# Stacking the two input parts into one 512-column product in half of a block's projections

## The chip, the cores and the metric

The kernel runs on one core of a Trainium2 chip. The core has five engines that run side by side and meet at semaphores: TensorE (PE in the profile, with its weight loads as PEld), VectorE (DVE), ScalarE (ACT), GpSimd (POOL) and SyncE (SP, which here only issues transfers). The metric is the device time of one execution in microseconds (us). Before the change the median of three runs is 792.66 us (792.65 to 792.79).

## What is computed

One layer of a streaming encoder on 256 frames (T = 256) of width 1024: a SwiGLU network, a mixing block, a cross-attention over a memory of 256 frames, and a second SwiGLU network. The mixing block is the part that matters here:

```
h = RMSNorm(x)
q_a, f_a, i_a, g_a, q_b, k_b, v_b, f_b, gates = split(h @ w_in)
A = gated linear recurrence of (q_a, f_a, i_a), 8 heads of 128
B = forgetting attention of (q_b, k_b, v_b, f_b), 8 heads of 128
y = sigmoid(gate_A) * (norm(A) * silu(g_a)) @ w_branch_a + sigmoid(gate_B) * B @ w_branch_b
x = x + RMSNorm(y @ w_out)
```

f_a are the forget gates, f = lb + (1 - lb) * sigmoid(f_a). The attention adds a running sum of log forget values to its scores. The cross-attention's queries are h @ w_mq, with h the next norm of x. Everything is float32.

## The kernel before

**Two parts for every operand.** TensorE is fed with numbers of a shorter float type (fp32r). Every operand is therefore split in two: hi is its rounded value, lo is what the rounding left. A product of x and w is the sum hi·hi + hi·lo + lo·hi, three products that accumulate in one PSUM bank. Weights arrive from memory as blocks of 128 x 1024 float32 (`load_split`, L130 to 145): SyncE issues the transfer into a `raw` tile, ScalarE casts it to `hi` (L142), VectorE subtracts to get `lo` (L144). There are four `raw` tiles and eight pairs of `hi` and `lo`; one *chunk* is four such blocks, the 1024 x 512 weights of 512 output columns. The activations' two parts lie in a class `Pair`: tiles `hT` and `lT`, transposed, with 256 frames as the free dimension. `gain_split` (L285, L286) writes them.

**Two kinds of projection.** `proj_tok` leaves frames on the partitions: 24 products of 512 columns for 128 frames and 512 outputs, the activations as the loaded operand. `proj_col` leaves outputs on the partitions: for 128 outputs and 256 frames, eight steps (kb) of three products of 256 columns, in which the weights are the loaded operand:

```python
MM(ps[:, a:b], wh, X.hi(kb)); MM(..., wh, X.lo(kb)); MM(..., wl, X.hi(kb))
```

`proj_col2` does this for two blocks of 128 outputs side by side in one PSUM bank of the ring `mm` (two banks). It is used for the forget gates f_a, the recurrence's queries q_a, the attention's k_b and q_b, the memory's keys mk and the memory queries mq. PSUM has eight banks in three rings: `mm` (2), `tr` (2, transposes) and `acc` (4).

**The order of the mixing block.** In the program's text: i_a; f_a (two chunks); q_a (two chunks); g_a with the attention's forget logit (three narrow chunks of 344 columns, `load_split(gf_in...)`); then k_b, q_b of the first four heads (c = 0) and k_b, q_b of the last four (c = 1); v_b; the gates; the branch projections. The recurrence is done in parallel over frames: class `Rec` (two of them, four heads each) builds products for distances 0, 1, 2, 4, ..., 128 in six *sets*, (0, 1), (2, 4), (8, 16), (32), (64), (128). Each set is: small products on TensorE into one or two `acc` banks (`products`), multiplications of K and Q in place on VectorE (`grow`, L705 and L715), copies by ScalarE of half of K (`gather`, L681) or of Q (`stash`, L685), and at the end `keep`, which copies the products out of PSUM into the score matrix (VectorE L729 and L734, ScalarE L743 to L751). A set needs the K and Q that the set before has grown. In the profile K is `k`, Q is `qf` (before its growth `q`), the gathered copy `early`, the small score matrix and the pairwise products of forget gates `aux` and `tq`, and the finished score matrix `f`. The sets stand in the text behind k_b and q_b, but with a mark: `after(r0 + R_AT[si])` with R_AT = (52, 126, 210, 254, 298, 344) gives them priority and lets them issue from that many products after the start of the g_a projection.

**What decides the order.** A planner takes the recorded instructions and lays each engine's list out by priority and by its estimate of when things are ready. A tile of a ring gets its buffer when an older tile of that ring has been released, and tiles of one ring get their buffers in the order of the text. Each engine then runs its list strictly in order.

**Behind the recurrence** stand the products of the score matrices with the inputs `iv` (called O below; L834 to 846: 24 products into four `acc` banks, which a norm and a product with `Gt`, L846, read), and the attention. Its scores are made in two groups of queries, each for two groups of heads, from k_b and q_b; VectorE adds the forget sums `cbc` and `cbm` (L883, L885). `cbm` is a broadcast of 8 x 256 numbers to 128 partitions, 512 KB, which GpSimd fetches (L857) and masks (L860); its tile takes a buffer of the general ring `m4`, and GpSimd's list holds the clearing of the score matrices (L723, `grow(1)`) ahead of it.

Of the kernel before, what the change touches and what calls it, by code (L numbers as in the profile page):

```python
# [11 lines left out]
F32 = mybir.dt.float32  # L12
F32R = mybir.dt.float32r
I32 = mybir.dt.int32
AF = mybir.ActivationFunctionType
ALU = mybir.AluOpType
AX = mybir.AxisListType

P = 128
D = 1024  # L20
T = 256
KB = D // P
# [57 lines left out]
def block_kernel(ctx: ExitStack, tc: tile.TileContext, wts, head_in, gf_in, x_in, mem_in, memT_in, cols, rows, fbias, masks, out):  # L80
    nc = tc.nc
    V, S, G, PE = nc.vector, nc.scalar, nc.gpsimd, nc.tensor
# [4 lines left out]
    sp = ctx.enter_context(tc.tile_pool(name="small", bufs=8))  # L87
# [5 lines left out]
    def MM(*args, **kw):  # L93
        log.append(PE.matmul(*args, **kw).ins)  # L94
# [9 lines left out]
    def nm(s):  # L104
        count[0] += 1
        return f"{s}_{count[0]}"

    def m4(shape, dt=F32, n="m"):
        return mp.tile(shape, dt, tag="m4", name=nm(n))
# [4 lines left out]
    def acc():  # L114
        return pp.tile([P, 512], F32, tag="acc", name=nm("acc"), bufs=4)

    def mm():
        return pp.tile([P, 512], F32, tag="mm", name=nm("mm"), bufs=2)
# [34 lines left out]
    def chunk(name, c):  # L153
        return [unit(name, 4 * c + i) for i in range(4)]

    def blk(units, kb, n=512):
        hi, lo = units[kb // 2]
        o = (kb % 2) * 512
        return hi[:, o : o + n], lo[:, o : o + n]

    def split(hi, lo, src):
        a = S.copy(hi, src)
        b = V.tensor_tensor(out=lo, in0=src, in1=hi.bitcast(F32), op=ALU.subtract)  # L163
        return a.ins, b.ins

    class Pair:


        def __init__(self, n=2):
            self.h, self.l = [], []  # L170
            for _ in range(n):
                self.more()
# [5 lines left out]
        def hi(self, kb, a=0, b=T):  # L178
            return self.h[kb // 4][:, kb % 4, a:b]

        def lo(self, kb, a=0, b=T):
            return self.l[kb // 4][:, kb % 4, a:b]

    def proj_tok(ps, X, units, h, n=512):

        a, b = h * P, h * P + P
        for kb in range(KB):
            wh, wl = blk(units, kb, n)
            MM(ps, X.hi(kb, a, b), wh, start=(kb == 0), stop=False)
            MM(ps, X.hi(kb, a, b), wl, start=False, stop=False)  # L190
            MM(ps, X.lo(kb, a, b), wh, start=False, stop=(kb == KB - 1))

    def proj_col(ps, X, units, cb):

        a, b = cb * P, cb * P + P
        for kb in range(KB):
            wh, wl = blk(units, kb)
            MM(ps, wh[:, a:b], X.hi(kb), start=(kb == 0), stop=False)
            MM(ps, wh[:, a:b], X.lo(kb), start=False, stop=False)
            MM(ps, wl[:, a:b], X.hi(kb), start=False, stop=(kb == KB - 1))  # L200

    def proj_col2(X, units, cbs):
        ps = mm()
        for j, cb in enumerate(cbs):
            proj_col(ps[:, j * T : (j + 1) * T], X, units, cb)
        return ps.rearrange("p (c t) -> p c t", c=2)

    def bc(a, shape, dim):
        return a.unsqueeze(dim).to_broadcast(shape)
# [54 lines left out]
    def fac_of(i, h):  # L264
        return fac[i][:, 32 * h : 32 * h + 1]
# [4 lines left out]
    def row_of(cols2):  # L270

        runs = sp.tile([P, 64], F32, tag="runs", name=nm("runs"), bufs=1)
        V.transpose(runs, cols2)
        rd = dp.tile([2, 4, 32], F32, name=nm("rd"))
        G.dma_start(rd.rearrange("h k t -> k h t"), runs[0:P:32].rearrange("k (h t) -> k h t", h=2))
        row = sp.tile([P, T], F32, tag="row", name=nm("row"), bufs=2)
        G.dma_start(row, rd.rearrange("h k t -> (h k t)").partition_broadcast(P))
        return row
# [204 lines left out]
    for kb in range(KB):  # L483
# [7 lines left out]
        if kb % 2 == 0 or kb == 1:  # L491
            a, b = ((0, 512), (512, D))[kb] if kb < 2 else (0, D)
# [8 lines left out]
    for kb in range(KB):  # L501
# [3 lines left out]
        for c in range(2):  # L505
            hi, lo = (p[:, kb % 2 * 512 : kb % 2 * 512 + 512] for p in cache[_AT["f1_in"] + 4 * c + kb // 2])
# [13 lines left out]
            nc.sync.dma_start(fb_s, fbias)  # L520
        return [rstd_x(x_halves(h)) for h in range(2)]

    X2 = Pair()
    r2 = [None, None]

    def half(X, r, h, g, *ms, into=None):

        for i, m in enumerate(ms):
            with after(m):
                to_T(X, x_blocks(h), h, g, (i,) if len(ms) == 2 else (0, 1))  # L530
        r[h] = rstd_x(x_halves(h), into)

    ffn("f1_in", "f1_dn", X1, norm_1, 0, 0, lambda m: half(X2, r2, 0, G_MIX, m + L_F1, into=fac_of(0, 0)))


    iv = [m4([P, 2, 512], n="iv") for _ in range(2)]
    for h in range(2):
        m = len(log)
        for c in range(2):
            ps = mm()  # L540
            if h == 0 and c == 1:
                behind.extend(evicted)
            u = chunk("i_a", c)
            behind.clear()
            proj_tok(ps, X2, u, h)
            iv_last = S.activation(iv[c][:, h, :], ps, AF.Copy, scale=r2[h]).ins
        if h == 0:
            half(X2, r2, 1, G_MIX, m + L_IA, into=fac_of(0, 1))
    row2 = row_of(fac[0])
# [18 lines left out]
    def heads_of(t, j):  # L568

        return t[:, :, 2 * j : 2 * j + 2].rearrange("p b h t -> p h b t")  # L570

    def halves(ps):
        return ps.rearrange("p h (b t) -> p h b t", b=2)

    row2h = row2.rearrange("p (b t) -> p b t", b=2)
    fT, kT_, qT_ = [], [], []
    for c in range(2):
        u = chunk("f_a", c)
        f, k = m4([P, 2, 4, P], n="f"), m4([P, 2, 4, P], n="k")
        for j in range(2):  # L580
            fj = heads_of(f, j)
            ps = proj_col2(X2, u, (2 * j, 2 * j + 1))
            V.tensor_tensor(out=fj, in0=halves(ps), in1=bc(row2h, [P, 2, 2, P], 1), op=ALU.mult)
            S.activation(fj, fj, AF.Sigmoid)
            for i in (2 * j, 2 * j + 1):
                hd = 4 * c + i
                V.tensor_scalar(out=f[:, :, i], in0=f[:, :, i], scalar1=olb[:, hd : hd + 1], scalar2=lbv[:, hd : hd + 1], op0=ALU.mult, op1=ALU.add)
        V.tensor_scalar(out=k, in0=f, scalar1=-1.0, scalar2=1.0, op0=ALU.mult, op1=ALU.add)
        fT.append(f)
        kT_.append(k)  # L590
    for c in range(2):
        u = chunk("q_a", c)
        q = m4([P, 2, 4, P], n="q")
        for j in range(2):
            qj = heads_of(q, j)
            ps = proj_col2(X2, u, (2 * j, 2 * j + 1))
            z = sp.tile([P, 2, 2, P], F32, tag="z2", name=nm("z2"), bufs=3)
            V.tensor_tensor(out=z, in0=halves(ps), in1=bc(row2h, [P, 2, 2, P], 1), op=ALU.mult)
            S.activation(qj, z, AF.Sigmoid)
            V.tensor_tensor(out=qj, in0=qj, in1=z, op=ALU.mult)  # L600
        qT_.append(q)
# [156 lines left out]
    for c in range(3):  # L758
        u = [load_split(gf_in[4 * c + i], GF) for i in range(4)]
        n = min(GF, D - c * GF)  # L760
        for h in range(2):
            ps = mm()
            proj_tok(ps[:, :GF], X2, u, h, GF)
            sg = sp.tile([P, 512], F32, tag="z2", name=nm("z2"), bufs=3)[:, :n]
# [31 lines left out]
    for c in range(2):  # L796
        for name, lst, sc in (("k_b", kb_, 1.0), ("q_b", qb_, 1.0 / math.sqrt(128.0))):
            u = chunk(name, c)
            t = m4([P, 4, T], n=name)
            m = len(log)  # L800
            for j in range(2):
                ps = proj_col2(X2, u, (2 * j, 2 * j + 1))
                for i in range(2):
                    V.scalar_tensor_tensor(out=t[:, 2 * j + i], in0=ps[:, i], scalar=sc, in1=row2, op0=ALU.mult, op1=ALU.mult)
            lst.append(t)
            if c == 0 and name == "k_b":
                forget(m + 46)
# [27 lines left out]
    for h in range(2):  # L835
        ps = [acc(), acc()]
        for hd in range(8):
            g, i = hd // 4, hd % 4
# [16 lines left out]
    for g in range(2):  # L855
        t = m4([P, 4, T], n="cbm")
# [68 lines left out]
    for c in range(2):  # L925
        u = chunk("v_b", c)
        t = m4([P, 2, 512], n="v_b")
        for h in range(2):
            ps = mm()
# [65 lines left out]
    for c in range(2):  # L995
        for name, X, zc in (("br_a", OA, c), ("br_b", OB, 2 + c)):
            u = chunk(name, c)
            for h in range(2):
                z = zs[zc][:, h]
                m = len(log)  # L1000
                ps = mm()
# [16 lines left out]
                for i, (xx, w) in enumerate(((X.hi(kb, a, b), wh), (X.hi(kb, a, b), wl), (X.lo(kb, a, b), wh))):  # L1018
                    MM(ps[n], xx, w[:, ns], start=(kb == 0 and i == 0), stop=(kb == KB - 1 and i == 2))

    X3 = Pair()
    r3 = [None, None]
    po = [[acc(), acc()], [acc(), acc()]]
    m = len(log)
# [11 lines left out]
    KM, QM, VM = Pair(0), Pair(0), Pair(0)  # L1036
    m = len(log)
    for c in range(2):
        u = chunk("mk", c)
        KM.more()  # L1040
        for j in range(2):
            js = slice(2 * j, 2 * j + 2)
            ps = proj_col2(M, u, (2 * j, 2 * j + 1))
            t = sp.tile([P, 2, T], F32, tag="z2", name=nm("km"), bufs=3)
            V.tensor_tensor(out=t, in0=ps, in1=bc(rowm, [P, 2, T], 1), op=ALU.mult)
            split(KM.h[c][:, js], KM.l[c][:, js], t)
            if j == 0:
                half(X3, r3, c, G_MEM, m + (L_WO, L_MK)[c], m + (L_WO, L_MK)[c] + 16)
    for c in range(2):
        u = chunk("mq", c)  # L1050
        QM.more()
        for j in range(2):
            js = slice(2 * j, 2 * j + 2)
            ps = proj_col2(X3, u, (2 * j, 2 * j + 1))
            split(QM.h[c][:, js], QM.l[c][:, js], ps)

    def mem_v(c):
        u = chunk("mv", c)
# [189 lines left out]
```

## Time and profile before

| | |
|---|---|
| median of 3 runs | 792.66 us |
| profiled execution | 792.24 us, its span 790.4 us |
| PE busy | 782.3 us, 4736 instructions |
| PEld busy | 677.6 us |
| DVE, ACT, POOL busy | 519.2, 426.7, 13.4 us |
| weights cast (L142), subtracted (L144) | 262.2 us of ACT, 306.6 us of DVE, 256 each |
| column products of 256 columns (`mm<-hT,hi`, `mm<-lT,hi`, `mm<-hT,lo`) | 384 of each: six projections, 48 blocks of 128 outputs, 8 steps each; 284 ns each as drawn |

The profile is one execution. The span runs from the first to the last instruction; the time of the execution is 1.84 us longer. A product's drawn length reaches into the next one, so the pitch (start to start) is what a product costs in a row of products, and it is read from the chain of waits, which cuts the execution into pieces of one engine. A product of two operands in plain float32 (the recurrence, the attention's scores) appears as two instructions.

### The profile page before, as it was taken

The numbers are of one execution on the slowest core, as the hardware profiler recorded it, in microseconds if no ns is written. First come the engines' busy times: TensorE is split into PE (matmuls) and PEld (weight loads), VectorE is DVE, ScalarE is ACT, GpSimd is POOL, SyncE is SP. The second block draws the span as 40 slices with busy tenths as digits, with TensorE's granted clock in tenths as the row PEclk, the third lists the DMA queues.
The fourth block names the chain that finished last, engine by engine and source line by source line (L and its number), as shares of the span: only waits on it lengthen the run. The fifth ranks groups of instructions, "written<-read, shape, count | busy, mean of one in ns | idle before, by whom it ended". The sixth has DMA issues, their size and how long they took to land.

```text
span 790.4 us, 12205 instructions
## 1 busy us (share of the span) xinstructions
PE 782.3 (99%) x4736; PEld 677.6 (86%) x4736; DVE 519.2 (66%) x826; ACT 426.7 (54%) x656; POOL 13.4 (2%) x36
## 2 busy tenths in 40 slices
PE   9999999999999999999999999999999999999996
PEld 7888888888899999998788888999888888888885
DVE  6774545557767899488686666964669754545543
ACT  7654444546664677357774345643647644444541
POOL 0000000000000102100000000000000000000000
PEclk9999999999999999999999999999999999999999
DMA  9775654563664547634576655455164655654521
GB/s 350 245 266 212 225 189 160 187 210 110 198 209 143 180 136 221 260 120 152 197 246 226 210 189 163 168 184 178 63 230 134 230 197 207 208 197 161 186 81 54
DMA packets 44345, 147.82 MB, mean 187 GB/s; under 512 B 5048, under 2 KB 8768, under 8 KB 44288
## 3 DMA queue, kind: packets, MB, share of 16 engines
q1 hardware_dynamic: 43168, 144.83, 53.9%
q0 software_dynamic: 688, 1.85, 0.9%
q8 instruction: 37, 0.61, 0.3%
q10 hardware_dynamic: 432, 0.37, 0.1%
q14 instruction: 20, 0.16, 0.1%
HBM read 145.97 MB, written 1.06 MB: 186 GB/s over the span
## 4 chain that ended last, share of the span: by engine, by line
PE 98%; DMA 1%; DVE 0%; ACT 0%; issue 0%; SPq 0%; DVEq 0%; ACTq 0%
PE mm L94 67%; PE acc L94 27%; PE tr L369 1%; PE tr L94 1%; PE tr L294 1%; DMA head<-in_head_dram 1%; PE tr L900 0%; PE tr L991 0%; PE acc L1101 0%; DVE xs L350 0%; DVE post L340 0%; ACT hi L509 0%; SPq L493 0%; ACT hT L285 0%; SPq L488 0%
## 5 line engine op out<-in xcount | busy, mean ns | idle before, releaser
L144 DVE TENSOR_TENSOR lo<-raw,hi 128x1024 fp32r<-128x1024 f32 (+1 forms) x256 | 306.6, 1206 | 122.4 <-ACT hi L142 114.3
L142 ACT CAST hi<-raw 128x1024 fp32r<-128x1024 f32 (+1 forms) x256 | 262.2, 1039 | 149.6 <-PE mm L94 82.2
L94 PE MATMUL mm<-lo,hT 128*128 128x512 f32 (+1 forms) x592 | 227.2, 386 | 0.0
L94 PE MATMUL mm<-hi,hT 128*128 128x512 f32 (+1 forms) x592 | 227.0, 386 | 0.0
L94 PE MATMUL mm<-hi,lT 128*128 128x512 f32 (+1 forms) x592 | 226.8, 386 | 0.0
L94 PEld LDWEIGHTS mm<-hi,hT 128*128 128x128 f32 x592 | 111.2, 188 | 21.4 <-ACT hT L285 0.3
L94 PEld LDWEIGHTS mm<-hi,lT 128*128 128x128 f32 x592 | 111.3, 188 | 21.4 <-DVE lT L286 0.2
L94 PEld LDWEIGHTS mm<-lo,hT 128*128 128x128 f32 x592 | 111.1, 188 | 20.6
L94 PE MATMUL acc<-hi,act 128*128 128x512 f32 x352 | 111.9, 391 | 0.0
L94 PE MATMUL mm<-hT,lo 128*128 128x256 f32 x384 | 109.2, 284 | 0.0
L94 PE MATMUL mm<-hT,hi 128*128 128x256 f32 x384 | 109.0, 284 | 0.0
L94 PE MATMUL mm<-lT,hi 128*128 128x256 f32 x384 | 109.0, 284 | 0.0
L94 PEld LDWEIGHTS acc<-hi,act 128*128 128x128 f32 x352 | 66.0, 188 | 13.6 <-DVE act L163 0.4
L94 PEld LDWEIGHTS mm<-hT,hi 128*128 128x128 f32 x384 | 73.7, 192 | 0.1
L94 PEld LDWEIGHTS mm<-lT,hi 128*128 128x128 f32 x384 | 73.7, 192 | 0.1
L94 PEld LDWEIGHTS mm<-hT,lo 128*128 128x128 f32 x384 | 73.7, 192 | 0.1
L94 PE MATMUL acc<-lo,act 128*128 128x512 f32 x176 | 69.8, 398 | 0.0
L374 ACT ACTIVATE sg<-mm,rstd 128x256 f32<-128x256 f32 x40 | 19.0, 475 | 75.5 <-PE mm L94 75.5
L379 DVE SCALAR_TENSOR_TENSOR at<-mm,rstd,sg 128x256 f32<-128x256 f32 x40 | 19.2, 480 | 57.4 <-ACT sg L374 57.4
L94 PEld LDWEIGHTS acc<-lo,act 128*128 128x128 f32 x176 | 33.1, 188 | 6.1
L94 PE MATMUL acc<-hi,hT 128*128 128x512 f32 x96 | 35.1, 392 | 0.7 <-ACT hi L509 0.4
L94 PE MATMUL acc<-hi,lT 128*128 128x512 f32 x96 | 35.1, 393 | 0.0
(199 smaller groups left out, 655.1 us busy)
## 6 DMA issues: line engine op xcount, KB each, us to landing
raw<-in_wts_dram SPq DMA_DIRECT2D x247, 512.0 KB, 4.4
raw<-in_gf_dram SPq DMA_DIRECT2D x12, 344.0 KB, 3.9
head<-in_head_dram SPq DMA_DIRECT2D x7, 392.0 KB, 6.5
grow<-in_rows_dram SPq DMA_DIRECT2D x4, 512.0 KB, 5.9
xs<-in_x_dram SPq DMA_DIRECT2D x2, 512.0 KB, 7.8
cbm<-cd POOLq DMA_DIRECT2D x2, 512.0 KB, 9.7
brow<-in_rows_dram SPq DMA_DIRECT2D x4, 256.0 KB, 4.9
memT<-in_memT_dram SPq DMA_DIRECT2D x2, 512.0 KB, 5.3
```

The lines of the kernel that those rows point to most:

```text
L94: log.append(PE.matmul(*args, **kw).ins)
L142: S.copy(h, r)
L144: V.tensor_tensor(out=l, in0=r, in1=h.bitcast(F32), op=ALU.subtract)
L294: PE.transpose(ps[:, j * P : (j + 1) * P], src(kb), ident)
L369: PE.transpose(trv[:, j, h * P : (h + 1) * P], ats[c, h][:, j * P : (j + 1) * P], ident)
L374: silu = S.activation(sg, ps[:, :FC], AF.Silu, scale=r2[h])
L379: V.scalar_tensor_tensor(out=a, in0=ps[:, FC:], scalar=r2[h], in1=sg, op0=ALU.mult, op1=ALU.mult)
```

## The change

Class `Joined` replaces `Pair` for the activations of the mixing block (X2) and of the memory queries (X3): the two parts of one kb lie side by side, so that `both(kb)` is 512 columns, hi then lo. `proj_both` multiplies the weights' first part with both in one product and the weights' second part with hi alone. One block of 128 outputs now takes a whole bank: its left half collects hi·hi + lo·hi, its right half the weights' first part times the activations' second. `added` puts them together. It is used for f_a, q_a, k_b and q_b of c = 1, and mq. k_b and q_b of c = 0 and mk stay with `proj_col2`. All of the new blocks take their bank from `acc`.

```diff
+    def proj_both(ps, X, units, cb):
+        a, b = cb * P, cb * P + P
+        for kb in range(KB):
+            wh, wl = blk(units, kb)
+            if kb == KB - 1:
+                MM(ps[:, :T], wl[:, a:b], X.hi(kb), start=False, stop=False)
+            MM(ps, wh[:, a:b], X.both(kb), start=(kb == 0), stop=(kb == KB - 1))
+            if kb < KB - 1:
+                MM(ps[:, :T], wl[:, a:b], X.hi(kb), start=False, stop=False)
+
+    def added(out, ps):
+        two = len(out.shape) == 3
+        lo = sp.tile([P, T], F32, tag="c1", name=nm("plo"), bufs=7)
+        S.copy(lo, ps[:, T:])
+        a, b = (t.rearrange("p (b t) -> p b t", b=2) if two else t for t in (ps[:, :T], lo))
+        V.tensor_tensor(out=out, in0=a, in1=b, op=ALU.add)
...
-    X2 = Pair()
+    X2 = Joined()
...
-            ps = proj_col2(X2, u, (2 * j, 2 * j + 1))
-            V.tensor_tensor(out=fj, in0=halves(ps), in1=bc(row2h, [P, 2, 2, P], 1), op=ALU.mult)
+            for i in (2 * j, 2 * j + 1):
+                ps = acc()
+                proj_both(ps, X2, u, i)
+                added(f[:, :, i], ps)
+            V.tensor_tensor(out=fj, in0=fj, in1=bc(row2h, [P, 2, 2, P], 1), op=ALU.mult)
...
-            ps = proj_col2(X2, u, (2 * j, 2 * j + 1))
             z = sp.tile([P, 2, 2, P], F32, tag="z2", name=nm("z2"), bufs=3)
-            V.tensor_tensor(out=z, in0=halves(ps), in1=bc(row2h, [P, 2, 2, P], 1), op=ALU.mult)
+            for i in range(2):
+                ps = acc()
+                proj_both(ps, X2, u, 2 * j + i)
+                added(z[:, i], ps)
+            V.tensor_tensor(out=z, in0=z, in1=bc(row2h, [P, 2, 2, P], 1), op=ALU.mult)
...
-                ps = proj_col2(X2, u, (2 * j, 2 * j + 1))
+                if c == 0:
+                    ps = proj_col2(X2, u, (2 * j, 2 * j + 1))
+                else:
+                    for i in range(2):
+                        ps = acc()
+                        proj_both(ps, X2, u, 2 * j + i)
+                        added(t[:, 2 * j + i], ps)
+                    ps = t[:, 2 * j : 2 * j + 2]
...
-    X3 = Pair()
+    X3 = Joined()
...
-        for j in range(2):
-            js = slice(2 * j, 2 * j + 2)
-            ps = proj_col2(X3, u, (2 * j, 2 * j + 1))
-            split(QM.h[c][:, js], QM.l[c][:, js], ps)
+        for i in range(4):
+            ps = acc()
+            proj_both(ps, X3, u, i)
+            hi, lo = QM.h[c][:, i], QM.l[c][:, i]
+            S.copy(hi, ps[:, :T])
+            t = sp.tile([P, T], F32, tag="c1", name=nm("qm"), bufs=7)
+            V.tensor_tensor(out=t, in0=ps[:, :T], in1=hi.bitcast(F32), op=ALU.subtract)
+            V.tensor_tensor(out=lo, in0=ps[:, T:], in1=t, op=ALU.add)
```

More of the change, by code (lines that the diff above doesn't have):

```diff
@@ L182, in lo, with __init__, hi, both @@
             return self.l[kb // 4][:, kb % 4, a:b]
+    class Joined:
+        def __init__(self):
+            self.t = [m4([P, 2, 2, T], F32R, "hlT") for _ in range(KB // 2)]
+        def hi(self, kb, a=0, b=T):
+            return self.t[kb // 2][:, kb % 2, 0, a:b]
+        def lo(self, kb, a=0, b=T):
+            return self.t[kb // 2][:, kb % 2, 1, a:b]
+        def both(self, kb):
+            return self.t[kb // 2][:, kb % 2].rearrange("p s t -> p (s t)")
+    def proj_both(ps, X, units, cb):
[13 more added lines that the diff above has]
+        V.tensor_tensor(out=out, in0=a, in1=b, op=ALU.add)
     def proj_tok(ps, X, units, h, n=512):
@@ L570, in heads_of @@
         return t[:, :, 2 * j : 2 * j + 2].rearrange("p b h t -> p h b t")
-    def halves(ps):
-        return ps.rearrange("p h (b t) -> p h b t", b=2)
     row2h = row2.rearrange("p (b t) -> p b t", b=2)
```

## The prediction

> **What bounds the kernel now.** I read the shares of busy time first, then the chain that ended last, then its pieces.
>
> ```profile
> PE 782.3 (99%) x4736; PEld 677.6 (86%) x4736; DVE 519.2 (66%) x826; ACT 426.7 (54%) x656; POOL 13.4 (2%) x36
> PEclk9999999999999999999999999999999999999999
> PE 98%; DMA 1%; DVE 0%; ACT 0%; issue 0%; SPq 0%; DVEq 0%; ACTq 0%
> ```
>
> PE works from 7.8 us to 783.8 us almost without a stop, at the full granted clock, and is 98% of the chain. So only two things can move the time: the pitch of PE's products, and stops of PE that are not there now. The pieces of the chain (start us, length us, what) that the sum needs:
>
> ```profile
> 45.14 10.90 PE mm L94 x48
> ...
> 268.53 1.81 PE acc L94 x122
> 270.34 11.87 PE mm L94 x74
> 282.21 1.28 PE acc L94 x86
> 283.49 8.50 PE mm L94 x64
> 292.00 0.22 PE tr L780 x2
> 292.21 2.38 PE mm L94 x20
> 294.60 1.33 PE acc L94 x108
> 295.92 5.46 PE mm L94 x44
> 301.39 0.69 PE acc L94 x50
> 302.08 5.46 PE mm L94 x44
> 307.55 1.08 PE acc L94 x32
> 308.63 5.71 PE mm L94 x46
> 314.34 1.79 PE acc L94 x16
> 316.13 21.95 PE mm L94 x183
> 338.08 5.36 PE acc L94 x48
> ...
> 347.09 0.22 PE tr L94 x2
> ...
> 497.82 7.66 PE mm L94 x64
> ```
>
> The six `acc` pieces from 268.53 to 314.34 are the recurrence's sets, 7.98 us together. Between two of them lie 11.87, 11.10, 5.46, 5.46 and 5.71 us of projection products, and in that time DVE and ACT grow K and Q without PE standing still.
>
> **What it removes.** 48 products of 512 columns take 10.90 us, a pitch of 0.2271; 64 products of 256 columns take 7.66, a pitch of 0.1197. A step kb was 3 x 0.1197 = 0.3591 and becomes 0.2271 + 0.1197 = 0.3468, so 0.0123 less. There are 32 changed blocks (f_a 8, q_a 8, k_b and q_b of c = 1 together 8, mq 8) with 8 steps each: 256 steps, **-3.1 us**. All of it lies on PE and so on the path. The Trainium skill, "TensorE: Matmul & The Clock Gate", section "Back-to-back issue gap", gives N / 2.4 + 2.5 ns for a product of N columns. By it the saving would be one fixed 2.5 ns per step, 0.64 us in all; the rows' pitches, 0.1197 and 0.2271, lie 10 to 11 ns above its 109.2 and 215.8, so the rows decide.
>
> **What it adds.** For 24 blocks ACT copies a half bank (128x256), DVE adds it, and DVE's multiplication by the row reads SBUF; mq has one ACT copy and two DVE operations per block. The nearest rows:
>
> ```profile
> L374 ACT ACTIVATE sg<-mm,rstd 128x256 f32<-128x256 f32 x40 | 19.0, 475 | 75.5 <-PE mm L94 75.5
> L804 DVE SCALAR_TENSOR_TENSOR k_b<-mm,row 128x256 f32<-128x256 f32 x8 | 3.0, 414 | 1.7 <-PE mm L94 1.7
> ```
>
> Per block 0.48 of ACT and 0.41 of DVE, in a time of 8 x 0.3468 = 2.77 us on PE. In the windows (us, then busy time of PE, PEld, DVE, ACT, POOL)
>
> ```profile
> 214.00:260.00 46.00, 46.00 (x385) 46.00 (x384) 32.03 (x45) 25.79 (x32) 0.00 (x0) 1.00 0.52 170
> ...
> 306.00:345.00 39.00, 39.00 (x346) 38.50 (x346) 25.73 (x41) 18.79 (x29) 6.41 (x10) 1.00 0.68 234
> ...
> 780.00:790.00 10.00, 3.76 (x17) 2.79 (x15) 3.57 (x10) 1.63 (x6) 0.00 (x0) 0.94 0.30 105
> ```
>
> f_a and q_a (the first) leave DVE 14 us and ACT 20 us free of 46, and four `acc` banks let a block wait three blocks, 8.3 us, for its eviction. I cost these at nothing; the bounds are 0 and one late eviction per chunk, 8 x 0.41 = 3.3. mq's last block is read by PE over 3 us after its end: nothing.
>
> **What it moves.** This decides. The new blocks take `acc` banks, and banks of a ring are given in the order of the text. The blocks of k_b and q_b with c = 1 stand in the text ahead of the recurrence's sets, so no set can have a bank until seven of these eight blocks have theirs. In the changed kernel's instruction list PE's order there is (products, kinds):
>
> ```
> 112+1 k_b, q_b c=1 | 96 sets 0,1 | 15 k_b, q_b | 16 | 3 v_b | 48 sets 2,4 | 10 v_b | 7 fox scores | 9 v_b
> | 64 sets 8,16 | 2 v_b | 16 | 1 v_b | 16 set 32 | 4 v_b | 8 set 64 | 14 v_b | 4 set 128 | 8 set 64 | 5 v_b
> | 4 set 128 | 1 fox score | 24 O | 21 v_b | ...
> ```
>
> Where 74, 84, 44, 44 and 46 products lay between the sets, there are now 18, 26, 3, 4 and 14. PE has little to do while DVE grows K and Q. The rows for that growth:
>
> ```profile
> 302.45 0.67 DVE L705 TENSOR_TENSOR k<-k,aux 128x512 f32<-128x512 f32 x1
> 303.05 0.67 DVE L705 TENSOR_TENSOR qf<-qf,aux 128x512 f32<-128x512 f32 x1
> ```
>
> ```profile
> L142 ACT CAST hi<-raw 128x1024 fp32r<-128x1024 f32 x24 | 24.2, 1046 | 19.0 <-PE mm L94 14.1 <-DMA raw<-in_wts_dram 4.8
> L681 ACT COPY early<-k 128x512 f32<-128x512 f32 x8 | 4.9, 636 | 1.8 <-DVE k L705 1.8
> L743 ACT COPY f<-aux 32x256 f32<-32x256 f32 x8 | 3.2, 403 | 0.1
> L748 ACT COPY f<-acc 64x256 f32<-64x256 f32 x4 | 1.5, 367 | 1.6 <-PE acc L94 1.6
> ```
>
> ```profile
> L734 DVE COPY_PREDICATED aux<-masks_s,acc 128x128 f32<-128x128 int32 x10 | 2.8, 368 | 0.0
> L885 DVE SCALAR_TENSOR_TENSOR p<-tr,ct,cbm 128x128 f32<-128x128 f32 x8 | 2.2, 341 | 0.7 <-issue 0.7
> ```
>
> One multiplication follows another after 0.60 us. With T0 the start of set 0 (near 324 us), by hand (estimates, each from these rows):
> - Sets 0, 1 end at 1.9. Eight multiplications (4.8) and two smaller products (0.7) later sets 2, 4 end at 7.4. PE's work in between is 15 products (2.55), 3 (0.68) and the sets' 1.28: idle **1.0**.
> - Sets 8, 16 need a bank that DVE frees with its copies of sets 0 and 1, 14 operations behind (eight at 0.60, the others near 0.3): 13.85, so the sets end at 15.35. Some ACT copies that DVE waits for stand behind weight casts of 1.05 us. Of these 7.95 us, PE fills 19 v_b products (4.31), 7 scores (1.54) and 1.33: idle **0.75**.
> - Set 32 ends at 17.55 behind its multiplications, PE filling 3 products and 0.69: **0.8**. The first half of set 64 ends at 19.3, filled by 4 products and 0.54: **0.3**.
> - At 19.1 DVE comes to the first addition with `cbm` (L885). On POOL's queue the fetch of `cbm` stands behind 12 clearings, and its buffer is that of the old q tile, which the products of set 8 read until 14.5:
>
> ```profile
> 271.91 3.05 POOL L723 MEMSET f<- 64x256 f32 x12 [63.72 <-ACT early L681]
> 310.57 1.10 POOL L857 DMA_DIRECT2D cbm<-cd  x2
> 318.95 1.27 POOL L860 TENSOR_SCALAR_AFFINE_SELECT cbm<-cbm 128x512 f32<-128x512 f32 x2 [7.28 <-DMA cbm<-cd]
> ```
>
> ```profile
> DMA to landing us min/median/max: 8.3/9.7/11.1
> ```
>
>  The clearings end by about 9. The fetch issues at 14.5, lands 8.3 later (the smaller value: the first of the two landed so), and two selections (1.27) make it 24.2. In DVE's queue the last multiplications for sets 64 and 128 wait behind that addition: four additions, a reduction, K and Q later, at 27.1, set 128 can start. PE's 14 products (3.2) end at 22.5: idle **4.85**.
> - Set 128 and the rest of set 64 end at 31.75: **0.95**. O waits for 13 ACT copies (0.37 to 0.40 each, from 29.6); with its 5.36 it ends at 38.8: **1.5**.
> - Behind it the second fox scores wait for O's banks, which the norm and L846 free, and their transposes for copies: **1.35**.
>
> The sum is 11.5 us of idle. PE's work is not changed by the moving. SP's list keeps its order; its transfers wait for `raw` tiles, which the casts among ACT's copies free, and the row below shows what each then needs. With four in flight I cost that at nothing, since PE's stops delay what reads the weights by as much; the bound is one transfer.
>
> ```profile
> raw<-in_wts_dram SPq DMA_DIRECT2D x247, 512.0 KB, 4.4
> ```
>
> Bounds of the idle: without the wait for `cbm` and with shorter hops 5.3; with a landing of 11.1 and 0.15 more on some 20 hops 17. A gain from the moving is excluded: PE now idles only at the two ends, 8 us together.
>
> **The sum.** The profiled execution took 792.24, 0.42 below the median. 792.24 - 3.1 + 11.5 = 800.6; against the median, **801.0**.
>
> **The rivals.**
> - *The recurrence still fits under its cover* (the other side). If the growth between sets ran beside v_b and the fox scores, with less than 1.5 us of idle, the saving would stay: 789.5 to 791. It decides at 3.1 us of idle. For it: PE never idled there before, and 48 v_b products (10.9) remain. Against: some 24 multiplications in a row at 0.60 are 14.4 us alone, and copies and `cbm` come on top. Chance 0.04; idle of 1.5 to 4.7, which gives within 0.2% of before (1.6 us, what a measurement of this kernel can tell), 0.03.
> - *The chain only*: `cbm` arrives in time, because the readers of the q tile end earlier or the fetch lands sooner, and no other wait takes its place: idle 5 to 8. For it: O could not start before ACT's 13 copies anyway. Against: what then ends last is again the chain of multiplications, and the waits behind O grow when it comes earlier. This gives 794.6 to 797.6. Chance 0.12.
> - *Longer*: the landing takes 11.1, the hops are slower, or the clock falls. In the window 780 to 790, where PE has stops, the granted clock is 0.94. If PE ran at half speed after its long stop, the 2.5 us of work behind it would double, less 0.95 idle that it fills: +1.6, 802.6; with the landing 805.4. The Trainium skill, same page, "Part 1: The HAM clock gate", says that a window of some 3.4 us without work halves the clock; this rule speaks against the change, and the 0.94 is the only trace of it here. Chance 0.19 for 803.5 to 807.
> - *The change doesn't do what it says*: 512 columns with two halves of one bank cost as much as two of 256 (no row shows a product of 512 into a bank that 256-column products also write): no 3.1, 804.1. It lies in the case before.
>
> **How the numbers follow.** The forecast, idle of 8 to 14 us, 797.6 to 803.5, has 0.60; the time is its middle, 801.0. Chain only 0.12, longer 0.19 (above 807 another 0.02), within 0.2% 0.03, faster 0.04. The range 795.0 to 806.4 takes in the two bounds of the idle (5.3 and 17, less 3.1) and leaves out some 0.13. Slower is 0.93.
>
> **What would show it.** Products of 512 columns into `acc` from hlT at a pitch of 0.227, and 4480 products in PE's count. PE's share of the chain under 98%, with DVE, ACT and POOL in it. Sets behind k_b and q_b in the chain, with PE idle between q_b and O: about 10 us in a stretch of 39. DVE idle before L885's addition, ended by POOL, some 5 us. The prediction falls if PE stays busy there, if the 3.1 is not seen before 300 us, or if the long stop has another cause than `cbm`.

## The result, and the profile after

The changed kernel takes 796.70 us (median of five runs, 796.49 to 798.06) against 792.66 before. The ratio is 1.0059 (95% interval 1.0048 to 1.0070): slower by 0.5 to 0.7%. The profiled execution took 796.49, with a span of 794.7.

The page of the changed kernel: PE's load, and the chain by engine.

```profile
PE 782.6 (98%) x4480; PEld 662.8 (83%) x4480; DVE 531.7 (67%) x862; ACT 434.2 (55%) x684; POOL 13.9 (2%) x36
PE 90%; DVE 5%; ACT 2%; issue 1%; DMA 1%; SPq 0%; POOL 0%; DVEq 0%; POOLq 0%; ACTq 0%
```

256 products are gone (4480 instructions), and PE's share of the chain has fallen from 98% to 90%. PE's busy time has not fallen, although it does less: a product is drawn longer than it takes (0.39 us for one of 512 columns, against a start-to-start time of 0.23), so a stop of 0.15 us behind a product is counted as busy.

PE's timeline shows where the recurrence's sets stand now (start, length, shapes; in brackets the idle time ahead and what ended it). Line numbers of the changed kernel are higher by 34 to 44 (L742 is L705 of before, L901 is L857, L929 is L885).

```profile
325.02 1.29 PE L94 MATMUL acc<-q,k 128*32 128x32 f32 x126
...
330.53 0.46 PE L94 MATMUL acc<-q,early 128*32 128x32 f32 x32 [0.87 <-ACT q L722]
...
341.36 0.46 PE L94 MATMUL acc<-qf,k 128*32 128x32 f32 x32 [0.27 <-DVE qf L742]
...
343.68 0.69 PE L94 MATMUL acc<-qf,k 128*64 128x64 f32 x16
...
348.40 1.77 PE L94 MATMUL acc<-qf,k 128*128 128x128 f32 x24 [0.63 <-DVE qf L742]
...
351.76 1.13 PE L94 MATMUL acc<-qf,k 128*128 128x128 f32 x8 [0.24 <-DVE qf L742]
...
355.48 1.35 PE L94 MATMUL acc<-iv,f 128*128 128x128 f32 x10 [1.09 <-issue]
...
359.94 0.48 PE L94 MATMUL mm<-hi,hlT 128*128 128x512 f32 x1
```

All six sets stand between 325 and 353, behind k_b and q_b. PE is drawn idle ahead of three of them (0.87, 0.27 and 0.63 us), inside the last (0.24) and inside O (1.09). In the kernel before, the same rows began at 268, and no stop of PE was drawn between 160 and 560 us.

The longer pieces of its chain around `cbm` (short ones between them are left out), and the answer on that tile:

```profile
337.06 2.09 PE mm L94 x9
339.15 0.44 PE acc L94 x32
339.63 0.48 issue
340.13 4.19 DMA cbm<-cd
344.46 0.63 POOL cbm L904
345.38 0.86 DVE p L929 x3
346.24 0.91 DVE k L742
347.15 0.59 DVE mx L930
347.74 0.61 DVE qf L742
348.40 1.17 PE acc L94 x8
```

```profile
L901 POOL DMA_DIRECT2D cbm<-cd x2: 547/552/558, 340.1 to 340.7; - x2
...
DMA to landing us min/median/max: 4.2/4.7/5.2
```

The end of set 8's products releases the fetch of `cbm`, the fetch releases the selections, these release DVE's additions, and behind them come the multiplications for set 128. Every link of the predicted chain is there; the landing took 4.2 us, half of the 8.3 that were forecast. The windows say why it could be quick:

```profile
306.00:325.00 19.00, 19.00 (x109) 16.28 (x107) 12.64 (x21) 7.20 (x12) 0.00 (x0) 1.00 0.65 222
325.00:340.00 15.00, 14.13 (x474) 11.83 (x475) 14.52 (x33) 11.04 (x18) 2.71 (x12) 1.00 0.02 4
340.00:360.00 20.00, 17.63 (x237) 14.35 (x223) 17.10 (x39) 15.03 (x46) 3.99 (x6) 1.00 0.30 107
```

The last two columns are the DMA engines' share and GB/s; the one ahead of them is the granted clock, 1.00 in all three. The weights' transfers had stopped (4 GB/s from 325 to 340), and `cbm` had the queues almost to itself. (It is two transfers of 512 KB, 1 MB in all, and not 512 KB.) In the kernel before, between 310.5 and 323 us, 2.58 MB of weights moved beside it, and `cbc`, another broadcast of 512 KB, had been issued 0.87 us ahead of it. In the five kernels of this document with late sets, the first of the two transfers lands in 4.2 to 4.4 us; in the eight with the sets among the products, in 7.9 to 9.3. No run changes the traffic alone, but one transfer speaks for the weights as the cause: in the changed kernel `cbc` is fetched at 296.85, with weights beside it and no other broadcast above 4 KB, and takes 8.3 us.

**How runs are compared below.** The first transfers land at different times: the first transposition of the first network starts at 32.0 to 34.2 us from one execution to the next, whatever the kernel. Two profiled executions are therefore compared from that instruction on. In the kernel before and the changed kernel it and the transpositions of G (`Gt`), which have the same work ahead of them in both, are these rows:

```profile
32.24 0.60 PE L369 MATMUL tr<-ident,at 128*128 128x128 f32 x4
...
371.48 1.03 PE L294 MATMUL tr<-ident,G 128*128 128x128 f32 x8
```

```profile
32.17 0.60 PE L403 MATMUL tr<-ident,at 128*128 128x128 f32 x4
...
376.09 1.03 PE L328 MATMUL tr<-ident,G 128*128 128x128 f32 x8
```

With the second transposition of X2's source (`xs`, near 200 us) and the last product of the second network, counted from that first row, in us:

| kernel | X2 | G | last product | against before |
|---|---|---|---|---|
| before | 168.32 | 339.24 | 751.13 | |
| changed | 169.00 | 343.92 | 755.47 | +4.34 |
| new tiles, old products | 169.00 | 339.88 | 752.06 | +0.93 |
| f_a, q_a, mq joined | 169.05 | 338.75 | 750.34 | -0.79 |
| changed, c = 1 in banks of mm | 168.98 | 338.15 | 749.78 | -1.35 |
| the same, tiles of kb and kb + 4 | 168.30 | 337.49 | 748.79 | -2.34 |

All kernels of the table are in the experiments. The +4.34 of the change comes apart into +0.93 for the new tiles, -2.28 for the products (749.78 against 752.06, same tiles and same order) and +5.69 for the late sets (755.47 against 749.78, same tiles and products).

### The profile page after: what moved, and what is told of

It reads as the page before. It is cut to its first block, busy times and chain, and to the rows that moved or that the text cites. A ratio compares the mean times of both kernels' runs of the same rounds, so it can differ in the third digit from the quotient of the medians.

```text
span 794.7 us, 11754 instructions
## 1 busy us (share of the span) xinstructions
PE 782.6 (98%) x4480; PEld 662.8 (83%) x4480; DVE 531.7 (67%) x862; ACT 434.2 (55%) x684; POOL 13.9 (2%) x36
## 4 chain that ended last, share of the span: by engine, by line
PE 90%; DVE 5%; ACT 2%; issue 1%; DMA 1%; SPq 0%; POOL 0%; DVEq 0%; POOLq 0%; ACTq 0%
PE mm L94 52%; PE acc L94 35%; PE tr L403 1%; DVE lo L144 1%; PE tr L94 1%; ACT junk L284 1%; PE tr L328 1%; DMA head<-in_head_dram 1%; DMA cbm<-cd 1%; DVE post L351 1%; ACT f L780 0%; DVE hlT L320 0%; PE tr L944 0%; DVE xs L355 0%; DVE k L742 0%
## 5 line engine op out<-in xcount | busy, mean ns | idle before, releaser
L94 PE MATMUL mm<-lo,hT 128*128 128x512 f32 x416 | 161.3, 391 | 0.0
L94 PE MATMUL mm<-hi,hT 128*128 128x512 f32 x416 | 161.1, 390 | 0.0
L94 PE MATMUL mm<-hi,lT 128*128 128x512 f32 x416 | 160.8, 390 | 0.0
L94 PE MATMUL mm<-hi,hlT 128*128 128x512 f32 (+1 forms) x352 | 104.2, 374 | 0.0
L94 PE MATMUL acc<-hlT,hi 128*128 128x512 f32 x256 | 88.3, 397 | 0.0
L94 PEld LDWEIGHTS mm<-hi,hlT 128*128 128x128 f32 x352 | 64.3, 188 | 9.6
L94 PE MATMUL acc<-hlT,lo 128*128 128x256 f32 x256 | 66.7, 281 | 0.0
L94 PE MATMUL mm<-lo,hlT 128*128 128x512 f32 (+1 forms) x176 | 65.8, 374 | 0.4 <-DVE lo L144 0.4
L94 PEld LDWEIGHTS acc<-hlT,hi 128*128 128x128 f32 x256 | 46.1, 188 | 8.7
L94 PEld LDWEIGHTS acc<-hlT,lo 128*128 128x128 f32 x256 | 48.3, 189 | 2.9
```

## The experiments

Theory A was that the late place of the recurrence's sets costs the time. Rival B was that the new products cost it, with their copies and additions.

**The place, with the products kept or left out.** First, c = 1 back to the old form:

```diff
-                if c == 0:
+                if True:
                     ps = proj_col2(X2, u, (2 * j, 2 * j + 1))
```

> k_b and q_b of c = 1 go back to two blocks of 256-column products in one bank of mm; f_a, q_a and mq stay joined. Theory A (the late place of the recurrence's sets costs the time, because the new blocks take acc banks ahead of them): the sets return to their old place, nothing stops PE there, and 192 steps save 0.0066 us each (0.3525 in the changed kernel's trace, 0.3591 before): 1.3 less, with up to 0.6 more for what delays PE near 198 us: 791.4 to 792.0. Rival B (the new products with their copies and additions cost the time, wherever they stand): three quarters of the added 4.0 us stay, 795.7.

Measured 791.79, ratio 0.9992 (0.9984 to 1.0001). Second, the new form in another ring:

```diff
                     for i in range(2):
-                        ps = acc()
+                        ps = mm()
                         proj_both(ps, X2, u, 2 * j + i)
```

> The changed kernel, but the joined blocks of k_b and q_b with c = 1 take their banks from the ring mm, one bank per block. All products, copies and additions are those of the changed kernel. Theory A: the sets stand in their old place and 256 steps save 0.0066 each, 1.7 less, with up to 0.6 near 198 us: 791.0 to 791.6. Rival B: as the changed kernel, 796.7, or more, since two banks wait for their evictions sooner than four.

Measured 791.60, ratio 0.9986 (0.9977 to 0.9995). One word takes away all that the change cost, with every product, copy and addition in place. B falls. Third, the sets late and nothing else changed, in the kernel before:

```diff
+                    for i in range(2):
+                        ps = acc()
+                        proj_col(ps[:, :T], X2, u, 2 * j + i)
```

> The kernel before with one edit: k_b and q_b of c = 1 take one acc bank per block of 128 outputs, with the old products and evictions. Theory A: the sets move as in the changed kernel and the saving is missing: 796.7 + 1.7, less up to 0.6 near 198 us: 797.8 to 798.4. Rival B: 792.7.

Measured 805.48, ratio 1.0156 (1.0141 to 1.0171). The direction is A's, but the loss is 7 us larger than A's number. PE's timeline of this kernel shows two stops that the changed kernel does not have, and its windows a granted clock of one half (the column behind POOL) for 3.4 and 6.8 us:

```profile
330.28 0.51 PE L94 MATMUL acc<-qf,early 128*32 128x32 f32 x35 [2.20 <-issue]
...
358.73 0.79 PE L94 MATMUL mm<-hi,hT 128*128 128x512 f32 x1 [3.04 <-ACT v_b L939]
359.32 0.63 PE L94 MATMUL mm<-lo,hT 128*128 128x512 f32 x1
```

```profile
331.01:334.43 3.42, 3.42 (x18) 3.42 (x18) 3.03 (x6) 2.81 (x5) 2.40 (x11) 0.50 0.02 5
358.32:365.14 6.82, 6.41 (x32) 5.12 (x33) 4.16 (x9) 5.36 (x18) 0.00 (x0) 0.50 0.04 5
334.43:358.32 23.89, 20.42 (x415) 15.76 (x413) 20.19 (x50) 13.01 (x30) 4.37 (x8) 1.00 0.20 68
```

The products from 331.09 to 334.08 start 0.21 us apart where 0.12 is usual, and those from 358.73 on 0.59 and 0.43 where 0.227 is usual. As an estimate from these rows, the two stops are 5.2 us and the half clock costs some 1.4 and 3.2 more, which covers the 7 us. This is the mechanism of the rival "longer". It did not happen in the changed kernel, whose longest drawn stop is 1.09, but it does in a kernel with nearly the same order. The Trainium skill, "TensorE: Matmul & The Clock Gate", "Part 1: The HAM clock gate", has a window of some 3.4 us without work for the halved clock; this trace agrees that the clock is halved, but the stops beside it were 2.20 and 3.04. Nor does the length of the stop alone decide it: a stop of 2.76 came with the half clock (c = 0 joined, below), while stops of 2.69 and 2.00 left it at 1.00 (`F_S` at 46, below). What ended the stop of 2.20 in the middle of a set's products the profile does not show.

**Why the sets were late.** The prediction's reason was that banks of a ring are given in the order of the text. It can be tried without another ring: the blocks of c = 1 move behind the sets in the text and keep `acc`.

```diff
-    for c in range(2):
+    def keys_queries(c):
...
+    keys_queries(0)
...            (the recurrence's sets)
+    keys_queries(1)
```

> The changed kernel with the blocks of k_b and q_b for c = 1 moved in the text behind the recurrence's sets; they keep their acc banks, their products and their weights. Theory A, as stated (a ring gives its banks in the order of the text, so the sets waited for these blocks): the sets go back to their old place and the time is that of the kernel with banks of mm, 0.9986 of before, 791 to 792. Rival (four acc banks are too few for the sets and the joined blocks, whatever their order): over 795.

Measured 792.62, ratio 0.9999 (0.9990 to 1.0008). The sets are back at their places among the products: counted from the first transposition, the first set starts at 236 us, as in the kernel before and in the one with banks of `mm`, against 293 in the changed kernel. Of the 0.6% that the change cost nothing is left. The time lies 0.6 us above the expected range, and in the trace the last product comes at 750.36, 0.58 behind the kernel with banks of `mm`; a stop of 0.25 ahead of set 128 is part of it. So the order of the text decides, and the choice of ring is second.

**The new tiles.** All products as before, the tiles of `Joined`:

```diff
-    X2 = Pair()
+    X2 = Joined()
...
-    X3 = Pair()
+    X3 = Joined()
```

> The kernel before with the two parts of the activations side by side in one tile, all products as before. Theory L (the new tiles make PE wait 0.4 to 0.6 us near 198 us): 793.1 to 793.3, with PE idle there. Rival: that wait comes from the products behind, and this kernel takes 792.7.

Measured 793.59, ratio 1.0018 (1.0010 to 1.0027), 0.3 us above theory L's range; the interval is clear of 1. ScalarE's timeline of this kernel where X2 is written, and PE's stop behind it:

```profile
188.42 0.35 ACT L300 ACTIVATE hlT<-tr,cols_s 128x128 fp32r<-128x128 f32 x1
189.34 0.37 ACT L300 ACTIVATE hlT<-tr,cols_s 128x128 fp32r<-128x128 f32 x1 [0.58 <-DVE hlT L301]
190.18 0.63 ACT L300 ACTIVATE hlT<-tr,cols_s 128x128 fp32r<-128x128 f32 x2 [0.47 <-DVE hlT L301]
...
193.79 2.93 ACT L142 CAST hi<-raw 128x1024 fp32r<-128x1024 f32 x3
```

```profile
198.69 0.50 PE L94 MATMUL mm<-lo,hlT 128*128 128x512 f32 x1 [0.38 <-DVE lo L144]
```

hi of the next step and lo of the step before now lie in one tile, and ScalarE's next write waits until VectorE has written. Four such waits (0.58, 0.47, 0.18, 0.49), where the kernel before has one of 0.18, push the weights' casts behind them back by 1.4 us, counted from the first transposition, and PE stops for a weight's second part. The remedy is to let neighbouring steps fall into different tiles:

```diff
-            return self.t[kb // 2][:, kb % 2, 0, a:b]
+            return self.t[kb % 4][:, kb // 4, 0, a:b]
```

> The changed kernel with another assignment of steps to tiles: a tile holds kb and kb + 4 in place of two neighbours, so that ScalarE's next hi and VectorE's last lo fall into different tiles. Theory L (in the changed kernel ScalarE waits for VectorE at every second hi, 1.7 us in all, which delays the weights' casts and subtractions near 190 us and stops PE at 198): PE does not stop there, 0.5 to 0.8 less: 795.9 to 796.2. Rival (the delay comes from elsewhere): 796.7 with the same stop.

Measured 796.94, ratio 1.0057 (1.0044 to 1.0070), against 1.0059 for the changed kernel. The times can't tell the two apart, and theory L's range was missed. In the trace ScalarE has a single wait of 0.17 at that place, as before, X2 comes at 168.33 as before, the stop at 198 is gone, and the last product comes at 755.13, 0.34 earlier than in the changed kernel: half of the 0.68 gained at X2 is lost further on, where PE stops for 0.65 us at 408.87 for a gate. With the sets in place nothing takes it back:

> Both edits: k_b and q_b of c = 1 take banks of mm, and a tile holds kb and kb + 4. Theories A and L together: 0.9986 of the time before in the run with mm alone, less 0.5 to 0.8: 790.4 to 791.2. If the tiles do not matter: 791.6.

Measured 790.25, ratio 0.9972 (0.9960 to 0.9983): faster than the kernel before by 0.2 to 0.4%, and no stop of PE is drawn between 160 and 560 us.

**The wait for `cbm`.** Moving the fox scores behind the recurrence in the lists takes the additions from ahead of the multiplications:

```diff
-F_S = 12
+F_S = 46
```

> The changed kernel with the first fox scores 34 products later (F_S 46 for 12), so that the additions which wait for cbm stand behind the last multiplications of K and Q in DVE's list; the sets stay late. Theory C (cbm in front of the multiplications costs time): in the changed kernel's trace DVE stands 1.1 us for it and the four additions and the reduction take 1.8 more ahead of the Q that set 128 needs; some 1 to 2.5 us go: 794.2 to 795.7. Rival: the multiplications and the copies alone set the end, and the 48 v_b products are used up ahead of it either way: 796.7, or up to 1 more.

Measured 801.46, ratio 1.0116 (1.0100 to 1.0132). Theory C missed, and the rival's range, up to 797.7, as well. Even the set that was to gain did not: set 128 starts 25.1 us after the first set's start, against 23.4 in the changed kernel, and the scores and their exponentials are late for what reads them. PE's timeline:

```profile
343.09 0.39 PE L94 MATMUL acc<-qf,early 128*32 128x32 f32 x21 [2.69 <-issue]
...
365.72 1.99 PE L94 MATMUL acc<-k_b,q_b 128*128 128x256 f32 x8 [0.84 <-DVE G L890]
...
394.80 0.66 PE L328 MATMUL tr<-ident,G 128*128 128x128 f32 x4 [0.55 <-DVE lT L320]
...
404.49 0.70 PE L94 MATMUL acc<-pT,v_b 128*128 128x256 f32 x2 [2.00 <-ACT pT L947]
```

The granted clock behind the two long stops:

```profile
343.09:350.00 6.91, 6.02 (x129) 4.14 (x130) 6.38 (x9) 2.39 (x9) 3.74 (x4) 1.00 0.26 97
404.49:412.00 7.51, 7.51 (x49) 6.42 (x49) 3.18 (x6) 2.59 (x6) 0.00 (x0) 1.00 0.70 237
```

The stop for `cbm` was exchanged for 2.69 us of which the profile names no cause, and for 2.00 at the attention's output. What the wait for `cbm` alone costs is not settled by this run.

**The pitch of wide and narrow products.**

```diff
-        for kb in range(KB):
+        for kb in range(0, KB, 2):
...            (two products with hi, two with lo)
```

> The changed kernel with the products of two steps grouped: two of 512 columns, then two of 256, so that wide and narrow products change half as often. In the changed kernel's trace a step takes 0.3525 us where the prediction had 0.3468. Theory D (each change between wide and narrow costs 3 ns): 0.3497 per step, 256 steps, 0.7 us less: 796.0. Rival (a wide product into a bank that narrow ones also write, or the load of its operand, costs this whatever the order): 0.3525 and 796.7.

Measured 798.12, ratio 1.0068 (1.0055 to 1.0082). The 256 products of f_a and q_a take 44.89 instead of 45.12, 0.3507 a step: 1.8 ns less, not the 2.8 of theory D. The whole is not faster: its ratio can't be told from the changed kernel's 1.0059. With the sets in place:

> The fastest kernel so far (banks of mm, a tile holds kb and kb + 4) with the products of two steps grouped, two wide and two narrow. In the late-set kernel grouping took a step of f_a and q_a from 0.3525 to 0.3507 us. Theory D: 256 steps, 0.46 less: 0.9966 of before, 789.8. Rival (what the pitch gains is lost at the blocks' borders, as the whole of the late-set kernel with grouping was not faster): 0.9972, 790.3.

Measured 790.12, ratio 0.9971 (0.9960 to 0.9983), not to be told from 0.9972 without grouping; the last product comes at 748.51, 0.28 earlier in the one trace.

**More of the same.** c = 0 joined as well, in banks of `mm`:

> The kernel with banks of mm and a tile holding kb and kb + 4, and k_b and q_b of c = 0 joined too: 8 more blocks. If the products count: 64 steps at 0.0066 to 0.009, 0.4 to 0.6 less than 0.9972, that is 0.9965 to 0.9967 (789.7 to 789.9). Rival (the copies and additions fall into the stretch near 290 us in which VectorE had no free time in the kernel before, 23.0 of 23.0 us, and delay the weights): 0.9972 or slower.

Measured 796.67, ratio 1.0057 (1.0044 to 1.0071). The rival was right that VectorE's stretch decides, and by far more than the 0.4 us at stake; but what waited was PE for a bank, and not the weights. PE's timeline:

```profile
292.15 0.47 PE L94 MATMUL mm<-hlT,hi 128*128 128x512 f32 x1 [1.36 <-DVE k_b L216]
...
308.05 0.80 PE L94 MATMUL mm<-hlT,hi 128*128 128x512 f32 x1 [2.76 <-DVE q_b L216]
```

The stretch (PE, PEld, DVE, ACT, POOL, granted clock) in the kernel before, then here, and here the time around the end of the second stop:

```profile
283.00:306.00 23.00, 23.00 (x411) 22.57 (x398) 23.00 (x47) 18.72 (x34) 0.39 (x1) 1.00 0.56 185
```

```profile
283.00:306.00 23.00, 20.91 (x239) 17.72 (x237) 21.55 (x47) 16.52 (x26) 0.11 (x1) 1.00 0.52 170
307.81:311.22 3.41, 3.17 (x10) 2.69 (x11) 2.32 (x5) 0.00 (x1) 1.72 (x2) 0.50 0.86 208
```

VectorE had no free time between 283 and 306 us before. Here each joined block asks it for an addition more, in a queue behind the growth of K and Q, and two banks of `mm` do not last until it comes: PE stops three times for these additions, 5.0 us in all. Around the end of the stop of 2.76 the granted clock is at half for 3.4 us, in which a step takes 0.64 us for 0.35; an estimate from these rows is some 1.5 us more.

## Why the prediction was right or wrong

The direction, the mechanism and the range (795.0 to 806.4) held. The time lies 4.3 us under the 801.0 that was forecast, and the case given 0.60 (idle of 8 to 14 us, 797.6 to 803.5) did not occur. The rival "the chain only" (0.12, 794.6 to 797.6) did, in the form "the fetch lands sooner".

Term by term, -3.1 and +11.5 were forecast; measured were -2.28 for the products, +0.93 for the tiles, which had no term, and +5.69 for the late sets. The first two errors add 1.75 us and hide a part of the third, 5.8 the other way. Without them the time would have been about 795.0, the lower end of the range: that it lies well inside is in part luck.

PE's timeline at the first product of f_a and the first of g_a, before and then changed:

```profile
213.93 0.28 PE L94 MATMUL mm<-hT,hi 128*128 128x256 f32 x1
...
260.00 0.32 PE L94 MATMUL mm<-hi,hT 128*128 128x344 f32 x1
```

```profile
214.54 0.39 PE L94 MATMUL acc<-hlT,hi 128*128 128x512 f32 x1
...
259.66 0.32 PE L94 MATMUL mm<-hi,hlT 128*128 128x344 f32 x1
```

- **The saving.** Forecast -3.1, measured -2.28 over 256 steps, 0.0089 a step for 0.0123. Between these two products the old form took 46.07 us for 128 steps (0.3599), the new one 45.12 (0.3525). The step's prices were both off: the narrow pitch there was 0.1200 and not 0.1197, and a wide product among narrow ones takes 0.23, not the 0.2271 of wide ones in a row. The rule that the prediction cites from the Trainium skill, "TensorE: Matmul & The Clock Gate", "Back-to-back issue gap", which the page gives for an isolated product, makes 0.64 us in all and was further from 2.28 than the rows. For f_a and q_a alone, 128 x 0.0074 is 0.95 of the 1.13 that they gave (G at 338.75 against 339.88 with the new tiles and old products); the remainder is not located.
- **The added copies and additions at nothing.** Right where they were placed: no stop of PE is drawn between 160 and 560 us in the kernel with both edits. The cover that was named, VectorE's free time, is real: with c = 0 in the stretch that has none, joining cost 6.4 us over that kernel (796.67 against 790.25, in ratios 1.0057 and 0.9972), its stops and the half clock together.
- **The tiles.** Costed at nothing because they were not looked at; +0.93. The prediction walked through the moved products and their queues, and not through who writes the new tile.
- **The late sets.** This step was worked out by hand, and its parts can be read against PE's timeline, from T0 = 325.02:

| end of, us after T0 | forecast | measured |
|---|---|---|
| sets 0, 1 | 1.9 | 1.8 |
| sets 2, 4 | 7.4 | 7.9 |
| sets 8, 16 | 15.35 | 15.3 |
| set 32 | 17.55 | 17.5 |
| set 64, first half | 19.3 | 19.3 |
| start of set 128 | 27.1 (27.35 by the idle that it counts) | 23.4 |
| sets 128, 64 | 31.75 | 27.7 |
| O | 38.8 | 34.9 |

 Up to the multiplications for set 64 the sum of rows (0.60 a multiplication, copies behind casts of 1.05) is right within 0.5 us. Then one term fails: *the landing of `cbm`, taken as 8.3, was 4.2*. The fetch, issued at 15.1 after T0 (forecast 14.5), was there at 19.3 and not at 22.8; DVE's first addition followed 0.8 later, behind one selection, and not 1.4 later behind two; and PE's 14 v_b products covered all but 0.63 of a stop forecast as 4.85. Both ends of the landing's bounds (8.3 and 11.1) came from a stretch with 234 GB/s on the queues, `cbm`'s own transfers included. The same step of the prediction said that PE would stop and the weights with it, and so had the reason for a quiet queue in hand.
- **What follows O** was 0.65 and not 1.35: 16.15 us from O's end to G's transpositions, for 53 products at 0.2271 and 3.46 of scores.
- **Idle in all.** By the prediction's rows, T0 to the end of O holds 28.65 of PE's work, so 6.25 of stops, and 0.65 behind: 6.9 for 11.5. Against the kernel with the sets in place the loss is 5.69. The remaining 1.2 fits what the sets cost PE there too: 44 products behind set 32 took 5.46 us before, where 44 at 0.1197 are 5.27, and similar behind the other sets. That share was only argued from the rows.
- **The other side** (the recurrence fits under its cover) fell as said. **The clock** stayed at 1.00 here, and fell in the kernel that only moves the sets.
- **The signs named in advance** came, but for two numbers: PE idle in the stretch was 6.3 and not 10, and DVE's wait ahead of L885's addition, ended by POOL, 1.1 and not 5. The wide products came at 0.23 and not 0.227. One sign against was badly chosen: of the 3.1, only the half of f_a and q_a could be seen before 300 us, as the joined blocks of k_b and q_b start at 305 and those of mq at 521. That half gave 1.13 for 1.57. The long stop for `cbm` was 0.63; the longest drawn stop, 1.09, is ahead of O's later products, where the chain has ACT's copies.

## What to carry to other kernels

Before costing an edit's arithmetic, ask which ring its results take and what stands behind it in that ring's order of allocation; here the word `acc` cost 5.7 us and the new products gave 2.3. A transfer's landing is read from the traffic that there will be, not the traffic that there was: here the edit itself emptied the queues, and the same transfer landed in half the time. And where two engines are made to write one tile, look at who waits for whom: giving neighbouring steps to different tiles cost nothing and, together with banks of `mm`, made the change worth 0.2 to 0.4%.

## What the runs showed of the hardware that was not expected

- A wide product between narrow ones has a pitch near 0.23 us against 0.2271 in a row of wide ones; two and two, the step of one wide and one narrow goes from 0.3525 to 0.3507.
- The granted clock fell to one half for 3.4 us beside stops of 2.20 and 2.76 us, and for 6.8 us beside one of 3.04. Stops of 2.69 and 2.00 us in another kernel, and of 1.36 and less, left it at 1.00. What decides between them is open.
- In two kernels with late sets PE stopped for 2.20 and 2.69 us in the middle of a set's small products, with no releaser that the profile shows ("issue"). In the kernels with the sets spread out this does not appear. The cause is open. A candidate that no run tests is PE's own instructions coming late: the queue that the profile calls `q8 instruction` has 37 transfers of 16 KB in the kernel before, for 4736 products and as many weight loads, and 35 in the changed one, for 4480 and as many, which is 256 instructions each; and such a transfer starts within 0.5 us of the start of both stops (at 327.62 and 340.79). Against it, the changed kernel has such transfers at its sets too (326.69, 341.03), and no stop there.
- A broadcast of 512 KB to 128 partitions landed in 4.2 to 4.4 us on nearly idle queues, and in 7.9 to 9.3 us with weights and another broadcast beside it.
